# Mixture-of-experts stage: order of the gather products, layout of the down weights, one more place in the weight ring

## The chip, the core and the metric

The kernel runs on one core of a Trainium2 chip. Its metric is the device time of one execution in microseconds. The core has TensorE (matmul, in the profile PE, its weight loads PEld), VectorE (DVE), ScalarE (ACT), GpSimd (POOL) and SyncE (SP); SP issues nearly all transfers from HBM, in its program's order. "MB" here is 1024 KB.

## The reference, cut to what matters

Two blocks over 256 tokens of 1024 columns in float32. The first block ends in a mixture of 32 experts of which each token takes four:

```python
hf = h.reshape(T, D)                                    # 256 x 1024
logits = hf @ w_router + b_router
top_val, top_idx = lax.top_k(logits, 4)
gates = jax.nn.softmax(top_val, axis=-1)
...
gu = xb @ w_gu[e] + b_gu[e]                             # rows of expert e; w_gu[e] is 1024 x 2048
g = jnp.minimum(gu[:, :1024], 7.0)
u = jnp.clip(gu[:, 1024:], -7.0, 7.0)
act = (u + 1.0) * (g * jax.nn.sigmoid(1.702 * g))
return act @ w_dn[e] + b_dn[e]                          # w_dn[e] is 1024 x 1024
...
y = jax.ops.segment_sum(out * row_gate, row_tok)        # back to the tokens, weighted by the gates
```

Ahead of it stand attention, a state-space mixer and their projections; behind it two further layers.

## The kernel before, in words

Each expert has 64 slots for its tokens; a token's slot is its rank among the expert's tokens, and `S` (built on VectorE, L1205) is the 0/1 matrix from tokens to the slots of two neighbouring experts (a pair). All experts are run, so the stage reads all weights: 256 loads of 1 MB of `w_gu` and 128 MB of `w_dn`.

**An expert**, in TensorE's order, which is written out by hand in `moe` (L1296 to L1313, kept by `in_order`):

- `gate_up(j, ...)` for j = 1 to 7 (j = 0 was done during the expert before): one load of 128 rows of `w_gu` (128 partitions x 2048 columns, 8 KB a partition), four matmuls of 128x64 against 128x512 into the accumulators `pg` and `pu` (L1361; the profile counts two instructions for each float32 matmul). After j = 2 and 3 it scatters the expert before back to the tokens (L1427 to L1430, added to `x` on VectorE). After j = 5 the bias is added (L1364).
- `turn`: the transposed slot matrix and the gates by slot (L1373, L1376).
- `rows` gathers half of the columns (four blocks of 128) of the next pair: for each block two products of `xn` and `S` into a quarter of the accumulator `hg_p` (L1214), then a ScalarE copy with scale and bias into `hg` (L1215). An even expert gathers blocks 0 to 3 of the next pair, an odd one blocks 4 to 7.
- `act`: the activation on VectorE and ScalarE (`swiglu`, L1098 to L1102), four transposes of its column blocks `act[:, q*128:(q+1)*128]` (L1387) and a ScalarE copy `aT` (L1389). The 64 slots of both column halves lie on 128 partitions, so block q holds rows 128q to 128q+127 of the upper half of the inner columns in one half of the partitions, and those of the lower half in the other.
- `gate_up(0, ...)` of the next expert.
- `down`: four loads of two row blocks of `w_dn` (L1395; partition p gets row p of each block, 4 KB apiece; the last expert cuts the fourth in two), 16 matmuls into `pdn` (L1399), then `out` on VectorE and ScalarE (L1413 to L1415).

Before expert 6 stands the bias of the down products (`down_bias`, L1320), before expert 18 a branch (`overflow`, L1446) that all engines take past code for experts with more than 64 tokens.

**Transfers.** A load takes the next place of a ring of 1 MB places (`slot`, L285; `ring_use`, L172) and is issued by SP when TensorE has released that place. The mixer leaves seven places, the pool `wr` five, the mixer's own tiles three, and `moe` opens `RF` = 4 more: 19. The four are the last in the ring's order. Loads of the first expert start while the mixer's last projections run.

**On-chip memory.** `e32` (softmax of the router's values), `Gx` and `no` (overflow) and `ov_o` have tiles of their own.

Of the kernel before, what the change touches and what calls it, by code (L numbers as in the profile page):

```python
# [8 lines left out]
F32 = mybir.dt.float32  # L9
# [3 lines left out]
AF = mybir.ActivationFunctionType  # L13
OP = mybir.AluOpType
AX = mybir.AxisListType
# [4 lines left out]
T, D, NB = 256, 1024, 2  # L20
# [1042 lines left out]
BS = 1  # L1063
# [6 lines left out]
BR = 1  # L1070
BW = 1
WY = 0
RF = 4
SP = ()
W0 = 0
LT = 0
# [10 lines left out]
NE = 32  # L1087
# [94 lines left out]
def moe(k):  # L1182
    nc, tc, i = k.nc, k.tc, k.i
    ctx = ExitStack()
    ps, sm = k.ps, k.phase(ctx, "smE", 0)
    M = ctx.enter_context(tc.tile_pool(name="moe", bufs=1, reuse_waits="tile"))
    w_gu, b_gu, w_dn, b_dn = i["w_gu"][0], i["b_gu"][0], i["w_dn"][0], i["b_dn"][0]
    k.ring(RF)
    k.anchor = k.after
    k.ring_use(RU, [n for n in range(len(k.more)) if n not in RU])  # L1190

    rs, lg, G, sel, rk, v8 = k.rsx, k.lg, k.G, k.sel, k.rk, k.v8
# [16 lines left out]
    def rows(S, hg, half):  # L1209

        p = ps.tile([128, 4, 2 * SLOTS], F32, name="hg_p", tag="at", bufs=2)
        for j in range(4 * half, 4 * half + 4):
            for b in range(NB):
                nc.tensor.matmul(p[:, j % 4], xn[:, b, j * 128:(j + 1) * 128], S[:, b], start=b == 0, stop=b == 1)  # L1214
            k.lastg = nc.scalar.activation(hg[:, j], p[:, j % 4], AF.Identity, scale=k.Af[:, j:j + 1], bias=k.Bf[:, j:j + 1]).ins  # L1215

    def room_rows():
# [23 lines left out]
    hold.__enter__()  # L1241


    e32 = sm.tile([128, NB, NE], F32, name="rt_e", bufs=1)
    s1 = sm.tile([128, NB], F32, name="rt_s", bufs=1)
    nc.vector.tensor_tensor(e32, lg, v8[:, :, 0:1].to_broadcast([128, NB, NE]), op=OP.subtract)
    nc.scalar.activation(e32, e32, AF.Exp)
    nc.vector.tensor_tensor(e32, e32, sel, op=OP.mult)
    nc.vector.tensor_reduce(s1, e32, axis=AX.X, op=OP.add)
    nc.vector.reciprocal(s1, s1)  # L1250
    nc.vector.tensor_tensor(G, e32, s1[:, :, None].to_broadcast([128, NB, NE]), op=OP.mult)
    pn = ps.tile([128, 32], F32, name="pn", tag="at", bufs=2)
    for b in range(NB):
        nc.tensor.matmul(pn, k.ones, sel[:, b], start=b == 0, stop=b == 1)
# [13 lines left out]
    for m in range(2):  # L1268
# [4 lines left out]
        p = ps.tile([128, 512], F32, name="pb", tag="at", bufs=2)  # L1273
# [10 lines left out]
    for e in range(NE):  # L1284
        q, u = e // 2, e % 2
# [54 lines left out]
class Expert:  # L1340
# [41 lines left out]
    def act(self):  # L1382
        k, nc = self.k, self.k.nc
        act = swiglu(k, self.M, self.pg, self.pu, WE[0] if self.final else 0)
        pt = k.ps.tile([128, 4, 2, 64], F32, name="pat", tag="tr", bufs=2)
        for q in range(4):
            k.tr(pt[:, q].rearrange("p a s -> p (a s)"), act[:, q * 128:(q + 1) * 128])  # L1387
        self.aT = self.M.tile([128, 4, 2, 64], F32, name="aT", tag="su", bufs=BSU)
        nc.scalar.activation(self.aT, pt, AF.Copy, scale=0.5)  # L1389

    def down(self):
        k, nc, e = self.k, self.k.nc, self.e
        self.pd = pd = k.ps.tile([128, 512], F32, name="pdn", tag="at", bufs=2)
        for j0, jn in ((0, 2), (2, 2), (4, 2), (6, 1), (7, 1)) if self.final else ((0, 2), (2, 2), (4, 2), (6, 2)):
            w = k.load([(lambda t: t, self.w_dn[e, j0 * 128:(j0 + jn) * 128, :].rearrange("(k p) c -> p k c", p=128))],  # L1395
                       [128, jn, 1024])
            for j in range(j0, j0 + jn):
                for c in range(2):
                    nc.tensor.matmul(pd[c * 64:c * 64 + 64], self.aT[:, j % 4, j // 4], w[:, j - j0, c * 512:(c + 1) * 512],  # L1399
                                     start=j == 0, stop=j == 7)  # L1400
# [39 lines left out]
def overflow(k, M, xn, G, rk, cnt, cmi):  # L1440

    nc, tc, i = k.nc, k.tc, k.i
    ps, sm = k.ps, k.sm
    w_gu, b_gu, w_dn = i["w_gu"], i["b_gu"], i["w_dn"]
    go = nc.values_load(cmi[0:1, 0:1], min_val=0, max_val=T)
    with tc.If(go > SLOTS):  # L1446
        Gx = M.tile([128, NB, NE], F32, name="Gx")
        no = M.tile([128, 1], F32, name="no")
        nc.vector.tensor_scalar(Gx, rk, float(SLOTS), None, op0=OP.is_gt)
        nc.vector.tensor_tensor(Gx, Gx, G, op=OP.mult)  # L1450
        nc.vector.memset(no, 0.0)
        hF = k.slot([128, 8, 256], "ov_h")
        for j in range(8):
            p = ps.tile([128, 256], F32, name="ov_x", tag="at", bufs=2)
            for b in range(NB):
                k.tr(p[:, b * 128:(b + 1) * 128], xn[:, b, j * 128:(j + 1) * 128])
            nc.scalar.activation(hF[:, j], p, AF.Identity, scale=k.Af[:, j:j + 1], bias=k.Bf[:, j:j + 1])
        with tc.For_i(0, NE, 1) as e:
            nc.vector.tensor_scalar(no, no, 1.0, None, op0=OP.add)
            ce = nc.values_load(cnt[0:1, bass.ds(e, 1)], min_val=0, max_val=T)  # L1460
            with tc.If(ce > SLOTS):
                aT = k.slot([128, 8, 256], "ov_a")
                for f in range(2):
                    pp = [[ps.tile([128, 512], F32, name="ov_p", tag="mm", bufs=4) for b in range(NB)] for m in range(2)]
                    for m in range(2):
                        c0 = m * 1024 + f * 512
                        br = M.tile([1, 512], F32, name="ov_w", tag="st", bufs=BST)
                        nc.sync.dma_start(br, b_gu[0, bass.ds(e, 1), c0:c0 + 512])
                        for b in range(NB):
                            nc.tensor.matmul(pp[m][b], k.ones[0:1], br, start=True, stop=False)  # L1470
                        for j in range(8):
                            w = M.tile([128, 512], F32, name="ov_w", tag=("sg", "su", "st")[j % 3], bufs=(BSG, BSU, BST)[j % 3])
                            nc.sync.dma_start(w, w_gu[0, bass.ds(e, 1), j * 128:(j + 1) * 128, c0:c0 + 512]
                                              .rearrange("o p c -> p (o c)"))
                            for b in range(NB):
                                nc.tensor.matmul(pp[m][b], hF[:, j, b * 128:(b + 1) * 128], w, start=False, stop=j == 7)
                    for b in range(NB):
                        act = swiglu(k, M, pp[0][b], pp[1][b])
                        pt = ps.tile([128, 4, 128], F32, name="ov_t", tag="tr", bufs=2)
                        for q in range(4):  # L1480
                            k.tr(pt[:, q], act[:, q * 128:(q + 1) * 128])
                        nc.scalar.activation(aT[:, f * 4:f * 4 + 4, b * 128:(b + 1) * 128], pt, AF.Copy, scale=0.5)
                gc = sm.tile([128, NB], F32, name="ov_g", bufs=1)
                for b in range(NB):
                    oh = sm.tile([128, 32], F32, name="ov_o", bufs=2)
                    nc.vector.scalar_tensor_tensor(oh, k.c("iota")[:, 0:32], no, Gx[:, b], op0=OP.is_equal, op1=OP.mult,
                                                   accum_out=gc[:, b:b + 1])
                for c in range(2):
                    pd = [ps.tile([128, 512], F32, name="ov_d", tag="mm", bufs=4) for b in range(NB)]
                    for j in range(8):  # L1490
                        w = M.tile([128, 512], F32, name="ov_w", tag=("st", "su")[j % 2], bufs=(BST, BSU)[j % 2])
                        nc.sync.dma_start(w, w_dn[0, bass.ds(e, 1), j * 128:(j + 1) * 128, c * 512:(c + 1) * 512]
                                          .rearrange("o p c -> p (o c)"))
                        for b in range(NB):
                            nc.tensor.matmul(pd[b], aT[:, j, b * 128:(b + 1) * 128], w, start=j == 0, stop=j == 7)
                    gr = M.tile([128, 512], F32, name="ov_r", tag="sg", bufs=BSG)
                    nc.sync.dma_start(gr, bass.AP(tensor=k.gfd.tensor, offset=k.gfd.offset + c * 512, ap=[[0, 128], [1, 512]]))
                    for b in range(NB):
                        t = M.tile([128, 512], F32, name="ov_y", tag="su", bufs=BSU)
                        nc.vector.scalar_tensor_tensor(t, pd[b], gc[:, b:b + 1], gr, op0=OP.mult, op1=OP.mult)  # L1500
                        xx = k.x[:, b, c * 512:(c + 1) * 512]
                        nc.vector.tensor_tensor(xx, xx, t, op=OP.add)
# [559 lines left out]
```

## Time and profile before

| what | value |
|---|---|
| median of 3 runs | 2073.04 us (2069.82 to 2073.42) |
| the profiled execution | 2070.68 us |
| its span, first to last instruction | 2068.9 us |
| mean granted TensorE clock | 0.970 of full |
| busy: PE / PEld / DVE / ACT / POOL | 1913.7 / 1232.0 / 1058.5 / 759.4 / 214.0 us |
| moved from HBM | 583.21 MB (here 10^6 bytes) in 204331 packets, 171424 of them under 8 KB |

The busy time of an engine is an average over stages with different limits. A slice of the page's second part is 1/40 of the span, 51.7 us; the expert stage lies in slices 8 to 26. A line of a timeline gives start, duration, engine, source line, operation, and in brackets the idle time before it and what ended it. A float32 matmul counts as two instructions.

### The profile page before, as it was taken

How to read it: one execution, taken by the hardware profiler on the slowest of the kernel's cores; microseconds unless marked ns; L12 is line 12 of the kernel's file. 1: busy time of each engine (PE TensorE's matmuls, PEld its weight loads, DVE VectorE, ACT ScalarE, POOL GpSimd, SP SyncE). 2: the span in 40 equal slices, each digit the busy share in tenths (PEclk: the TensorE clock that was granted, in tenths of full speed). 3: DMA queues.
4: the chain of work that ended last, by engine and by line, in shares of the span. 5: the costliest groups of instructions: out<-in, count | busy, mean ns of one | idle time of the engine just before them, and what ended most of it. 6: DMA issues, size and time to landing. Idle time of an engine off the chain costs nothing.

```text
span 2068.9 us, 28319 instructions
## 1 busy us (share of the span) xinstructions
PE 1913.7 (92%) x11058; PEld 1232.0 (60%) x11059; DVE 1058.5 (51%) x1916; ACT 759.4 (37%) x1477; POOL 214.0 (10%) x379
## 2 busy tenths in 40 slices
PE   6898999999999999979999999899899999989998
PEld 4777888333333333323333333477699977769996
DVE  3788665222322222212222222387789757778984
ACT  3647444211101111101111111246567644556763
POOL 1324300000000000000000000111112101011210
PEclk9899999999999999989999999899999999999999
DMA  9766457999999999999999999453255546335552
GB/s 335 243 222 219 158 189 292 363 417 417 416 389 418 416 416 418 416 380 417 415 416 417 417 416 416 155 184 102 82 184 184 174 140 205 102 102 170 179 176 98
DMA packets 204331, 583.21 MB, mean 282 GB/s; under 512 B 15080, under 2 KB 92408, under 8 KB 171424
## 3 DMA queue, kind: packets, MB, share of 16 engines
q1 hardware_dynamic: 203200, 578.32, 73.7%
q0 software_dynamic: 704, 1.98, 0.3%
q8 instruction: 89, 1.46, 0.3%
q10 hardware_dynamic: 288, 1.05, 0.1%
q14 instruction: 50, 0.41, 0.1%
HBM read 580.23 MB, written 1.07 MB: 281 GB/s over the span
## 4 chain that ended last, share of the span: by engine, by line
PE 46%; DVE 5%; ACT 2%; issue 2%; DMA 1%; POOL 0%; DVEq 0%; POOLq 0%; ACTq 0%
PE mm L340 8%; PE mm L341 8%; PE mm L339 8%; PE pg L1361 5%; PE pu L1361 5%; PE pdn L1399 5%; PE hg_p L1214 2%; DVE wL L328 1%; ACT hg L1215 1%; PE pc L1427 1%; DVE ac L1870 1%; PE apv L1851 1%; ACT wH L327 0%; PE warm L403 0%; PE apl L1829 0%
## 5 line engine op out<-in xcount | busy, mean ns | idle before, releaser
L328 DVE TENSOR_TENSOR wL<-w,wH 128x1024 fp32r<-128x1024 f32 (+1 forms) x241 | 307.1, 1275 | 125.7 <-ACT wH L327 121.9
L327 ACT ACTIVATE wH<-w 128x1024 fp32r<-128x1024 f32 x259 | 272.0, 1052 | 181.9 <-PE mm L340 78.0
L1361 PE MATMUL pg<-w,hg 128*64 128x512 f32 x1024 | 280.2, 626 | 9.9 <-DMA w<-in_w_gu_dram 9.9
L1361 PE MATMUL pu<-w,hg 128*64 128x512 f32 x1024 | 267.1, 598 | 0.0
L341 PE MATMUL mm<-hnH,wL 128*128 128x256 f32 x800 | 229.1, 286 | 1.2 <-POOL xp L1865 0.8
L1399 PE MATMUL pdn<-w,aT 128*64 128x512 f32 x1024 | 225.2, 592 | 1.4 <-ACT aT L1389 1.4
L339 PE MATMUL mm<-hnH,wH 128*128 128x256 f32 x800 | 226.4, 283 | 0.0
L340 PE MATMUL mm<-hnL,wH 128*128 128x256 f32 x800 | 226.2, 283 | 0.0
L1413 DVE SCALAR_TENSOR_TENSOR oe<-pdn,gs,gf 128x512 f32<-128x512 f32 x32 | 24.0, 750 | 384.5 <-PE pdn L1399 384.5
L1099 ACT ACTIVATE sw_t<-sw_g 128x512 f32<-128x512 f32 x32 | 20.2, 630 | 424.7 <-DVE sw_g L1098 424.7
L1361 PEld LDWEIGHTS pu<-w,hg 128*64 128x64 f32 x1024 | 75.7, 141 | 154.0 <-issue 154.0
L1399 PEld LDWEIGHTS pdn<-w,aT 128*64 128x64 f32 x1024 | 72.9, 137 | 147.7 <-issue 144.5
L341 PEld LDWEIGHTS mm<-hnH,wL 128*128 128x128 f32 x800 | 153.2, 191 | 3.5 <-DVE wL L328 1.3
L339 PEld LDWEIGHTS mm<-hnH,wH 128*128 128x128 f32 x800 | 153.3, 192 | 0.5 <-issue 0.4
L340 PEld LDWEIGHTS mm<-hnL,wH 128*128 128x128 f32 x800 | 153.3, 192 | 0.0
L1214 PE MATMUL hg_p<-S,xn 128*128 128x128 f32 x512 | 94.2, 310 | 50.9 <-ACT hg L1215 49.3
L1361 PEld LDWEIGHTS pg<-w,hg 128*64 128x64 f32 x1024 | 63.6, 140 | 126.4 <-issue 121.8
L1430 DVE TENSOR_TENSOR x<-x,pc 128x512 f32<-128x512 f32 x128 | 82.5, 684 | 106.7 <-PE pc L1428 106.7
L1414 ACT ACTIVATE oeH<-oe 128x512 fp32r<-128x512 f32 x32 | 20.2, 630 | 293.7 <-DVE oe L1413 293.7
L1214 PEld LDWEIGHTS hg_p<-S,xn 128*128 128x128 f32 x512 | 69.3, 197 | 71.3 <-ACT hg L1215 66.9
L341 PE MATMUL mm<-hH,wL 128*128 128x256 f32 x320 | 96.3, 302 | 10.4 <-DVE wL L328 10.4
L328 POOL TENSOR_TENSOR wHL<-w,wHL 128x1024 fp32r<-128x1024 f32 x1 | 2.4, 2357 | 966.9 <-ACT wHL L327 966.9
(543 smaller groups left out, 3509.2 us busy)
## 6 DMA issues: line engine op xcount, KB each, us to landing
w<-in_w_gu_dram SPq DMA_DIRECT2D x256, 1024.0 KB, 13.8
w<-in_w_dn_dram SPq DMA_DIRECT2D x127, 1024.0 KB, 16.0
w<-in_w_in_dram SPq DMA_DIRECT2D x51, 1024.0 KB, 5.6
w<-in_w_up_dram SPq DMA_DIRECT2D x44, 1024.0 KB, 5.1
w<-in_w_down_dram SPq DMA_DIRECT2D x20, 1024.0 KB, 5.0
ad_l<-in_w_ada_dram SPq DMA_DIRECT2D x32, 512.0 KB, 4.3
w<-in_w_out_dram SPq DMA_DIRECT2D x12, 1024.0 KB, 5.1
w<-in_w_ada_dram SPq DMA_DIRECT2D x8, 1024.0 KB, 9.8
```

The source lines that it names most:

```text
L327: self.nc.scalar.activation(H, w, AF.Copy)
L328: (eng or self.nc.vector).tensor_tensor(L, w, H.bitcast(F32), op=OP.subtract)
L339: nc.tensor.matmul(out, sH, mH, start=start, stop=False, **kw)
L340: nc.tensor.matmul(out, sH, mL, start=False, stop=False, **kw)
L341: return nc.tensor.matmul(out, sL, mH, start=False, stop=stop, **kw)
L1214: nc.tensor.matmul(p[:, j % 4], xn[:, b, j * 128:(j + 1) * 128], S[:, b], start=b == 0, stop=b == 1)
L1215: k.lastg = nc.scalar.activation(hg[:, j], p[:, j % 4], AF.Identity, scale=k.Af[:, j:j + 1], bias=k.Bf[:, j:j + 1]).ins
L1361: nc.tensor.matmul(p[o:o + 64], hg, w[:, n * 512:(n + 1) * 512], start=j == 0, stop=j == 7 and e > 0)
L1399: nc.tensor.matmul(pd[c * 64:c * 64 + 64], self.aT[:, j % 4, j // 4], w[:, j - j0, c * 512:(c + 1) * 512], start=j == 0, stop=j == 7)
L1413: nc.vector.scalar_tensor_tensor(oe, self.pd, self.gs, k.gf, op0=OP.mult, op1=OP.mult)
L1427: nc.tensor.matmul(p, self.ST[o, b], self.oH[o], start=True, stop=False)
L1430: dx = nc.vector.tensor_tensor(xx, xx, p, op=OP.add)
```

## The change

- In `rows` the eight products of a half come first, then its four copies.
- `down` gives each partition two neighbouring rows of a 256-row block (8 KB in one piece in HBM) in place of one row from each of two 128-row blocks. So that products and weights meet, the transposes take every second column of a 256-column block: `act[:, c:c+255:2]`.
- `RF` goes from 4 to 5: 20 places.
- Memory for it: the softmax works in place in `G`; `Gx` and `no` take rooms of tiles that exist; `ov_o` has one buffer.

```diff
-RF = 4
+RF = 5
...
         for j in range(4 * half, 4 * half + 4):
             for b in range(NB):
                 nc.tensor.matmul(p[:, j % 4], xn[:, b, j * 128:(j + 1) * 128], S[:, b], start=b == 0, stop=b == 1)
+        for j in range(4 * half, 4 * half + 4):
             k.lastg = nc.scalar.activation(hg[:, j], p[:, j % 4], AF.Identity, scale=k.Af[:, j:j + 1], bias=k.Bf[:, j:j + 1]).ins
...
-    e32 = sm.tile([128, NB, NE], F32, name="rt_e", bufs=1)
...
-    nc.vector.tensor_tensor(e32, lg, v8[:, :, 0:1].to_broadcast([128, NB, NE]), op=OP.subtract)
-    nc.scalar.activation(e32, e32, AF.Exp)
+    nc.vector.tensor_tensor(G, lg, v8[:, :, 0:1].to_broadcast([128, NB, NE]), op=OP.subtract)
+    nc.scalar.activation(G, G, AF.Exp)
...
         for q in range(4):
-            k.tr(pt[:, q].rearrange("p a s -> p (a s)"), act[:, q * 128:(q + 1) * 128])
+
+            c = q // 2 * 256 + q % 2
+            k.tr(pt[:, q].rearrange("p a s -> p (a s)"), act[:, c:c + 255:2])
...
         for j0, jn in ((0, 2), (2, 2), (4, 2), (6, 1), (7, 1)) if self.final else ((0, 2), (2, 2), (4, 2), (6, 2)):
-            w = k.load([(lambda t: t, self.w_dn[e, j0 * 128:(j0 + jn) * 128, :].rearrange("(k p) c -> p k c", p=128))],
-                       [128, jn, 1024])
+            r = j0 // 2 * 256
+            src = self.w_dn[e, r:r + 256, :].rearrange("(p k) c -> p k c", k=2)
+            w = k.load([(lambda t: t, src[:, j0 % 2:j0 % 2 + jn])], [128, jn, 1024])
...
-        Gx = M.tile([128, NB, NE], F32, name="Gx")
-        no = M.tile([128, 1], F32, name="no")
+        Gx = M.tile([128, NB, NE], F32, name="Gx", tag="ST", bufs=BS)
+        no = M.tile([128, 1], F32, name="no", tag="gs", bufs=2)
...
-                    oh = sm.tile([128, 32], F32, name="ov_o", bufs=2)
+                    oh = sm.tile([128, 32], F32, name="ov_o", bufs=1)
```

## Rows read from the trace of the kernel before

**Rows 1.** Page, part 2: GB/s of the DMA engines in 40 slices.
```profile
GB/s 335 243 222 219 158 189 292 363 417 417 416 389 418 416 416 418 416 380 417 415 416 417 417 416 416 155 184 102 82 184 184 174 140 205 102 102 170 179 176 98
```

**Rows 2.** Waits of SP, whole span: us in total, times, longest.
```profile
SPq L301 <- PE pu L1361: 422.0, 177, 8.9
...
SPq L301 <- DMA w<-in_w_gu_dram: 82.0, 51, 2.4
```

**Rows 3.** TensorE timeline at expert 18: start, us, operation [idle before <-releaser].
```profile
912.28 1.12 PE L1361 MATMUL pg<-w,hg 128*64 128x512 f32 x2 [9.90 <-DMA w<-in_w_gu_dram]
```

**Rows 4.** ScalarE timeline, activation of experts 9, 10, 11 and 31.
```profile
649.38 0.63 ACT L1099 ACTIVATE sw_t<-sw_g 128x512 f32<-128x512 f32 x1 [12.86 <-DVE sw_g L1098]
...
678.06 0.63 ACT L1099 ACTIVATE sw_t<-sw_g 128x512 f32<-128x512 f32 x1 [12.86 <-DVE sw_g L1098]
...
708.36 0.63 ACT L1099 ACTIVATE sw_t<-sw_g 128x512 f32<-128x512 f32 x1 [12.86 <-DVE sw_g L1098]
...
1304.95 0.63 ACT L1099 ACTIVATE sw_t<-sw_g 128x512 f32<-128x512 f32 x1 [12.86 <-DVE sw_g L1098]
```

**Rows 5.** SP timeline, last expert load; landing of the issues from 1276 to 1284.
```profile
1281.45 2.09 SPq L301 DMA_DIRECT2D w<-in_w_dn_dram  x1
...
DMA to landing us min/median/max: 17.3/18.3/20.1
```

**Rows 6.** TensorE and VectorE timeline, end of expert 31.
```profile
1308.75 7.09 PE L1399 MATMUL pdn<-w,aT 128*64 128x512 f32 x32 [0.69 <-ACT aT L1389]
...
1315.89 0.75 DVE L1413 SCALAR_TENSOR_TENSOR oe<-pdn,gs,gf 128x512 f32<-128x512 f32 x1 [8.60 <-PE pdn L1399]
```

**Rows 7.** Timeline: a gather inside expert 0, then expert 1's, all engines.
```profile
359.53 1.16 PE L1214 MATMUL hg_p<-S,xn 128*128 128x128 f32 x8
360.62 1.08 PE L1361 MATMUL pg<-w,hg 128*64 128x512 f32 x4
...
409.22 0.46 ACT L1215 ACTIVATE hg<-hg_p,Bf,Af 128x128 f32<-128x128 f32 x1 [0.43 <-PE hg_p L1214]
...
409.73 0.71 PE L1214 MATMUL hg_p<-S,xn 128*128 128x128 f32 x4 [0.55 <-ACT hg L1215]
...
410.02 0.69 DVE L1102 SCALAR_TENSOR_TENSOR sw_t<-sw_t,sw_u 128x512 f32<-128x512 f32 x1
...
412.80 0.60 PE L407 MATMUL pat<-cst,sw_t 128*128 128x128 f32 x4
...
413.44 0.60 ACT L1389 ACTIVATE aT<-pat 128x512 f32<-128x512 f32 x1
...
415.10 7.04 PE L1399 MATMUL pdn<-w,aT 128*64 128x512 f32 x32
```

**Rows 8.** Waits of TensorE, whole span.
```profile
PE hg_p L1214 <- ACT hg L1215: 49.3, 90, 0.6
```

**Rows 9.** TensorE timeline behind the gather of expert 5.
```profile
530.18 1.12 PE L1361 MATMUL pg<-w,hg 128*64 128x512 f32 x2
```

**Rows 10.** SP timeline, four issues in a row late in the stage.
```profile
1235.92 0.33 SPq L301 DMA_DIRECT2D w<-in_w_gu_dram  x1
...
1238.48 0.33 SPq L301 DMA_DIRECT2D w<-in_w_gu_dram  x1
...
1241.01 0.33 SPq L301 DMA_DIRECT2D w<-in_w_gu_dram  x1
...
1243.50 0.38 SPq L301 DMA_DIRECT2D w<-in_w_dn_dram  x1
```

**Rows 11.** Stretches: us, busy us (instructions) of each engine, PEclk, DMA share, GB/s.
```profile
360.00:370.00 10.00, 10.00 (x57) 4.67 (x57) 1.66 (x8) 2.93 (x7) 0.00 (x0) 1.00 0.91 323
380.00:390.00 10.00, 8.35 (x46) 4.19 (x47) 1.39 (x4) 2.52 (x6) 0.00 (x0) 1.00 0.52 201
570.00:580.00 10.00, 10.00 (x48) 3.23 (x46) 1.44 (x2) 0.63 (x1) 0.00 (x0) 1.00 0.80 293
900.00:910.00 10.00, 1.84 (x5) 0.79 (x4) 2.48 (x4) 0.00 (x0) 0.00 (x0) 0.55 0.61 224
```

More of the change, by code (lines that the diff above doesn't have):

```diff
@@ L1241, in moe @@
     hold.__enter__()
-    e32 = sm.tile([128, NB, NE], F32, name="rt_e", bufs=1)
     s1 = sm.tile([128, NB], F32, name="rt_s", bufs=1)
-    nc.vector.tensor_tensor(e32, lg, v8[:, :, 0:1].to_broadcast([128, NB, NE]), op=OP.subtract)
-    nc.scalar.activation(e32, e32, AF.Exp)
-    nc.vector.tensor_tensor(e32, e32, sel, op=OP.mult)
-    nc.vector.tensor_reduce(s1, e32, axis=AX.X, op=OP.add)
+    nc.vector.tensor_tensor(G, lg, v8[:, :, 0:1].to_broadcast([128, NB, NE]), op=OP.subtract)
+    nc.scalar.activation(G, G, AF.Exp)
+    nc.vector.tensor_tensor(G, G, sel, op=OP.mult)
+    nc.vector.tensor_reduce(s1, G, axis=AX.X, op=OP.add)
     nc.vector.reciprocal(s1, s1)
-    nc.vector.tensor_tensor(G, e32, s1[:, :, None].to_broadcast([128, NB, NE]), op=OP.mult)
+    nc.vector.tensor_tensor(G, G, s1[:, :, None].to_broadcast([128, NB, NE]), op=OP.mult)
     pn = ps.tile([128, 32], F32, name="pn", tag="at", bufs=2)
```

## The prediction, made before the changed kernel ran

> **What bounds the kernel now.** I read the slices of the span first, then the expert stage alone: intervals between experts, waits of TensorE, waits of the DMA queue, spacing of its issues, stretches of 10 us. In the slices the expert stage is the plateau near 417 GB/s [rows 1]. The weights are 384 MB, the rate hardly leaves that plateau, and one would call the stage bound by transfers. It is not. SP waits for release of a place by TensorE (422.0 us in 177 waits) far more than for an earlier transfer (82.0 us) [rows 2]: the ring is full and TensorE empties it. TensorE waits for weights once in the stage, 9.90 us at the branch before expert 18 [rows 3], where all engines jump over the overflow code; I read that wait as the jump's and expect it to stay.
>
> TensorE's pace is in the start times of one ScalarE instruction that each expert issues once: 649.38 to 678.06 is 28.68 us, 678.06 to 708.36 is 30.30 us [rows 4]. Of the 31 intervals eight are of the long kind, 1.63 us longer. Twelve transfers of about 2.5 us are 30.1 us, so TensorE eats weights faster than they come. It never starved because its own stalls (the bias step after expert 5, the branch, the long intervals) let the ring fill again. At the end the last half megabyte is issued near 1281.5; the last four loads take 17.3 us and more to land [rows 5], so it is there at about 1299. TensorE is done with it at 1315.9 [rows 6]. Some 16 us of slack is therefore all that TensorE can gain before transfers take over, plus what transfers themselves can gain.
>
> **The change, part by part.**
>
> *Gather first, copies behind.* Now each of the four groups of products waits 0.55 us for the copy of the one before, and groups start 1.26 us apart; expert 0's first gather, where nothing waits, shows eight instructions in 1.09 us, 0.545 a group [rows 7]. Thirty gathers have 90 such waits, 49.3 us [rows 8]. Without them a gather is 4 x 0.545 = 2.2 us instead of 3 x 1.26 + 0.55 = 4.3, so 2.1 us shorter. What comes next may be late: the transposes need the activation, ready at 410.02 + 0.69 = 410.71, and products would end at 408.47 + 2.2 = 410.67 (the group before the row at 409.73 began 1.26 earlier): no loss. Then ScalarE has four copies of 0.46 us in a row, 1.84 us, and the copy of the transposed activation behind them: it would start near 412.7 and end near 413.3. The down products want to start 2.30 us behind the transposes (415.10 less 412.80), at 413.0 [rows 7]. So 0.3 to 0.6 us go back; where this copy has no cover now, TensorE waits 0.69 us for it [rows 6]. I take 1.7 us an expert; the ends are 0.5 (the copies also start late and cover nothing) and 2.1 (they start early).
>
> *The clock.* The long intervals have a stretch right behind the gather where two matmul instructions of 128x512 take 1.12 us [rows 9]; 32 of that shape take 7.09 us at the end of the stage [rows 6], 0.44 for two, so this is the lower level, 1.2 GHz. TensorE had just idled 0.55 of each 1.26 us. With the idle gone I take these eight as gone, 8 x 1.63 = 13 us; the other end is that all stay, 0.
>
> TensorE's own demand thus falls by 30 x 1.7 + 13 = 64 us, past the slack. From there transfers decide, so their sum is the forecast.
>
> *Two rows to a partition.* Late in the stage landings pace the issues: each issue waits for the landing of the one eight places back (up to 20.1 us in flight [rows 5], at 2.5 us each). The issues of the last gate-up loads thus show down-weight landings, 2.56 and 2.53 us apart, and the first down issue follows at 2.49, a gate-up landing [rows 10]. Gate-up rows are 8 KB in one piece, down rows 4 KB. The change makes down weights 8 KB a partition; I take 2.49 for them: 0.065 x 4 x 30 experts = 8 us less transfer time. Ends: 0 (the pieces stay 4 KB) and 9. The price is the transposes reading every second column. No row shows such a read of a stationary operand; the bounds are 0 and a doubling of the 0.60 us group [rows 7]; I take 0, and with 0.6 TensorE still has some 2 us an expert in hand against transfers.
>
> *The twentieth place.* It puts one more transfer, 2.5 us, in front while the ring is full. Against 417 GB/s the stretches 360 to 370, 380 to 390, 570 to 580 and 900 to 910 lose 2.3, 5.2, 3.0 and 4.6 us of transfer time [rows 11], because TensorE released nothing for a while. Of the first two the extra place regains 2.5 and the shorter gather 1.7. The other two vanish: by then TensorE is further ahead and some eight transfers are queued, and the same two stalls don't drain them. Sum 4.2 + 3.0 + 4.6 = 11.8 us; ends: 8 (only the later two) and 15 (all).
>
> *The rest.* In-place softmax issues the same instructions and ends long before its gate is read by the first expert. The overflow tiles lie in code that is jumped over. The extra place is the last in the ring's order, so a late release of its memory would delay only the load that now waits for expert 0 anyway. No load's queue or order changes otherwise.
>
> *Sum.* Last landing 1299 - 8 - 11.8 = 1279. The last gate-up load lands four transfers (10 us) earlier; behind it TensorE has one step of 1.7 us, 3.8 us to the down products (1304.95 [rows 4] to 1308.75), and 7.1 us of these [rows 6], which ends 2.6 us behind the last landing. I add 1.5 us because TensorE works off a few landed loads at that point. End 1283 instead of 1315.9: 33 us. The layers behind it start 33 us earlier with unchanged work; their first load is next in the same queue. The profiled execution took 2070.68 us, span 2068.9: 2070.7 - 33 = 2038. The median shown is 2.4 us above that execution, so I state 2038 with the spread of such runs inside the range.
>
> **The rivals.**
>
> *Down pieces stay as they are* (their two rows not joined into one piece): 8 us fewer, 2046. For it: nothing in the trace shows joined rows. Against: each partition's two rows are adjacent on both sides.
>
> *The wait only moves and TensorE stays the bound*: saving 0.5 us an expert and the clock still falling, 30 x 0.5 = 15 us, 2056. For it: ScalarE's four copies now stand ahead of the one that the down products need. Against: these have 2.3 us of cover.
>
> *Nothing*: the tool that orders the instructions keeps the copies interleaved or the strided transposes eat the gain; 2070.
>
> *Slower: the clock.* Once TensorE is ahead it waits for weights in each expert, about 29.8 - 27.0 = 2.8 us. If that drops the clock twice in each expert at 1.63 us, TensorE takes 30 x (3.3 - 1.7) = 47 us more, less the 13 us of drops that it has now: 34 us slower, 2105. It decides from 1.3 drops an expert (2.1 us saved, the present drops among it, over 1.63). For it: after the 9.9 us idle at the branch the granted clock of that stretch was 0.55 [rows 11], and gathers with 44% idle drop it in eight cases. Against: those gathers did not in 23 others, and a slowed TensorE stops waiting, so the cause removes itself. The Trainium skill (TensorE: Matmul & The Clock Gate, "HAM oscillation") says that a loop which computes for less time than it waits for its next weights is throttled again in every tile; by that rule the risk is real only where waits are longer than the work, which no row before shows: here the wait would be 2.8 of 29.8 us. I leave it 9 in 100.
>
> **How the numbers follow.** Transfers become the bound: 0.66, 2031 to 2044, likeliest 2038. Pieces stay: 0.10. Wait moves: 0.10. Nothing: 0.05. Clock: 0.09. The range 2030 to 2058 holds the first three and leaves out the last two; its low end is the sum of the better ends (15 + 9 regained, nothing to work off: 2032) less 2 us for the spread of runs. Changes of under 0.2% (4 us) are what this measurement can't tell from none: faster 0.86, same 0.05, slower 0.09.
>
> **What would show it.** The waits of the gather products for ScalarE are gone and groups are 0.55 us apart; intervals start near 27 us and settle near 29.8 once waits for gate-up weights of 2 to 3 us appear in each expert. SP waits for landings rather than releases in the second half; issues are 2.49 apart throughout; packets under 8 KB become fewer. The last load lands near 1279, the last down products end near 1283. I am wrong if intervals stay at 28 us or more from the start (moved wait, clock), if TensorE never waits for weights, or if the half-speed stretches multiply.

## The result, and the profile after

The changed kernel takes 2042.49 us (median of 4 runs, 2040.89 to 2043.66) against 2071.43 us of the kernel before (4 runs, 2066.49 to 2073.42) beside it on the same chip: a ratio of 0.986 [0.985, 0.988], 29 us less. The forecast was 2038 and 33 us; the result lies in the range, and in the direction and the case (transfers become the bound) that were called likeliest. The profiled execution took 2042.99 us with a span of 2041.3.

First the page, the GB/s of the 40 slices and the packets:

```profile
GB/s 339 238 228 211 167 179 288 390 420 421 420 420 420 420 420 420 421 375 420 420 420 420 420 420 420 241 145 93 82 213 177 176 153 191 104 83 176 187 175 93
...
DMA packets 188075, 583.21 MB, mean 286 GB/s; under 512 B 15080, under 2 KB 92408, under 8 KB 138912
```

Against [rows 1] the expert stage has one dip left (375, the branch); the dip of 389 is gone, and the plateau stands at 420 instead of 417. The packets fit the two rows to a partition: under 8 KB there are 138912, and 171424 where the down weights have the old layout (the page of the kernel with the order alone, below).

Next the waits, of SP (three rows) and of TensorE: us in total, times, longest.

```profile
SPq L301 <- DMA w<-in_w_gu_dram: 449.6, 215, 3.2
...
SPq L301 <- DMA w<-in_w_dn_dram: 224.8, 105, 6.0
...
SPq L301 <- PE pu L1361: 67.6, 41, 8.7
...
PE pg L1361 <- DMA w<-in_w_gu_dram: 20.7, 40, 0.7
```

SP's waits have changed sides [rows 2]: 422.0 us for TensorE's release became 67.6, and 82.0 us for an earlier gate-up transfer became 449.6, with 224.8 for down transfers. TensorE waits for gate-up weights 40 times, half a microsecond on average and never over 0.7 us. Its 90 waits for a copy inside a gather [rows 8], three in each of 30 gathers, are gone.

The timeline of the stage, in order of time: start, us, engine and operation [idle before it, and what ended it].

```profile
354.59 5.44 PE L1214 MATMUL hg_p<-S,xn 128*128 128x128 f32 x32 [1.40 <-DVE S L1205]
...
571.89 2.05 PE L1214 MATMUL hg_p<-S,xn 128*128 128x128 f32 x16
...
573.98 1.51 ACT L1216 ACTIVATE hg<-hg_p,Bf,Af 128x128 f32<-128x128 f32 x4 [1.77 <-PE hg_p L1214]
...
574.27 0.72 PE L407 MATMUL pat<-cst,sw_t 128*128 128x128 f32 x4 [0.33 <-DVE sw_t L1102]
...
575.36 0.61 ACT L1391 ACTIVATE aT<-pat 128x512 f32<-128x512 f32 x1
...
576.68 1.89 PE L1402 MATMUL pdn<-w,aT 128*64 128x512 f32 x8
...
624.43 0.63 ACT L1099 ACTIVATE sw_t<-sw_g 128x512 f32<-128x512 f32 x1 [12.86 <-DVE sw_g L1098]
...
651.28 0.63 ACT L1099 ACTIVATE sw_t<-sw_g 128x512 f32<-128x512 f32 x1 [12.86 <-DVE sw_g L1098]
...
677.60 0.63 ACT L1099 ACTIVATE sw_t<-sw_g 128x512 f32<-128x512 f32 x1 [12.85 <-DVE sw_g L1098]
...
862.33 0.33 SPq L301 DMA_DIRECT2D w<-in_w_gu_dram  x1
...
864.83 0.33 SPq L301 DMA_DIRECT2D w<-in_w_dn_dram  x1
...
867.34 0.33 SPq L301 DMA_DIRECT2D w<-in_w_dn_dram  x1
...
1216.36 0.63 ACT L1099 ACTIVATE sw_t<-sw_g 128x512 f32<-128x512 f32 x1 [15.82 <-DVE sw_g L1098]
...
1246.47 0.63 ACT L1099 ACTIVATE sw_t<-sw_g 128x512 f32<-128x512 f32 x1 [16.05 <-DVE sw_g L1098]
...
1276.36 0.63 ACT L1099 ACTIVATE sw_t<-sw_g 128x512 f32<-128x512 f32 x1 [14.82 <-DVE sw_g L1098]
...
1280.25 7.09 PE L1402 MATMUL pdn<-w,aT 128*64 128x512 f32 x32 [0.69 <-ACT aT L1391]
...
1287.39 0.75 DVE L1416 SCALAR_TENSOR_TENSOR oe<-pdn,gs,gf 128x512 f32<-128x512 f32 x1 [8.68 <-PE pdn L1402]
```

What to see in it: the gather inside expert 7 (571.89) is one group of 2.05 us where [rows 7] had groups 1.26 us apart. The four copies take 1.51 us together, and the copy of the transposed activation ends at 575.97, ahead of the down products at 576.68, so these do not wait for ScalarE. The transposes wait 0.33 us for the activation here. Four transposes with the stride take 0.72 us, where [rows 7] had 0.60. The intervals between the activations are 26.85 and 26.32 us around 650 us, where [rows 4] had 28.68 and 30.30, and 30.11 and 29.89 at the end, where transfers pace. SP's issues around a down piece are 2.50 and 2.51 us apart; [rows 10] had 2.56 and 2.53. The last down products begin at 1280.25 instead of 1308.75 [rows 6], 28.5 us earlier, and that is the gain: from there to the end both profiles take about as long (760.2 and 761.1 us of their spans).

Now the stretches that [rows 11] showed, with 370 to 380 beside them and the 100 us around the branch; the last two columns are the DMA share and GB/s, the one before them the granted clock:

```profile
360.00:370.00 10.00, 10.00 (x45) 3.51 (x46) 2.30 (x11) 2.82 (x8) 0.00 (x0) 1.00 1.01 389
...
370.00:380.00 10.00, 10.00 (x61) 4.66 (x58) 2.33 (x6) 1.50 (x3) 0.00 (x0) 1.00 0.96 375
...
380.00:390.00 10.00, 9.95 (x51) 3.92 (x51) 0.51 (x1) 1.99 (x5) 0.00 (x0) 1.00 0.97 351
...
570.00:580.00 10.00, 9.67 (x68) 5.21 (x66) 3.39 (x9) 2.95 (x7) 0.00 (x0) 1.00 1.01 418
...
900.00:910.00 10.00, 1.47 (x6) 1.02 (x8) 2.74 (x5) 2.63 (x7) 0.00 (x0) 0.50 0.56 206
...
860.00:960.00 100.00, 77.90 (x368) 29.79 (x366) 19.02 (x35) 7.74 (x17) 0.00 (x0) 0.85 0.96 398
```

Between 360 and 390 us the transfers now lose 3.4 us against 420 GB/s; before, they lost 2.3 and 5.2 in the two stretches of [rows 11] against 417, and 0.5 in the one between them (396 GB/s). The dip at 570 to 580 is gone. The one at 900 to 910 is still there: 206 GB/s, and 398 instead of 420 over 100 us, so 5.2 us lost. This is the branch before expert 18, seen by its own line (first and last start of each kind, then who waited for it):

```profile
L1449 SPq EVENT_SEMAPHORE  x9: 17/17/17, 890.6 to 905.3; - x9
...
L1449 PEldq COMPARE_BRANCH  x1: 5989/5989/5989, 868.3 to 868.3; - x1
...
L1449 SPq COMPARE_BRANCH  x1: 50/50/50, 885.5 to 885.5; - x1
...
  DVE sw_g L1098: 16.5, 1
```

SP reaches its branch at 885.5, has a last event there at 905.3, and issues nothing in those 20 us. That is how long one piece takes to land with eight on the way: its last issue ahead of the branch was near 885, and 19.9 us is the median landing time of a gate-up piece on the page. The events are those of the join, the point behind the skipped code where SP goes on. Of SP's waits from 880 to 912 us the join takes 19.4 us, and a release by TensorE 0.3 us:

```profile
SPq L1449 <- SPq L1449: 19.4, 3, 11.8
```

The drain costs the transfers less than its 20 us, because the eight pieces on the way still land. The rate is full until about 899 us, falls while the queues run empty, and is full again at 908:

```profile
904.00:905.00 1.00, 0.00 (x0) 0.00 (x0) 0.00 (x0) 0.00 (x0) 0.00 (x0) 0.50 0.02 8
...
908.00:909.00 1.00, 0.47 (x3) 0.50 (x3) 0.39 (x1) 0.61 (x2) 0.00 (x0) 0.50 1.03 434
```

DVE's first step of expert 18 waits 16.5 us, until SP's join is over, TensorE's transposes wait for DVE (13.6 us), and the interval of this expert is 54.6 us.

### The profile page after: what moved, and what is told of

Read it like the earlier page. It is cut to its first block, busy times and chain, and to the rows that moved or that the text cites. A ratio compares the mean times of both kernels' runs of the same rounds, so it can differ in the third digit from the quotient of the medians.

```text
span 2041.3 us, 28318 instructions
## 1 busy us (share of the span) xinstructions
PE 1899.5 (93%) x11058; PEld 1223.8 (60%) x11059; DVE 1057.7 (52%) x1916; ACT 746.4 (37%) x1477; POOL 215.3 (11%) x379
## 2 busy tenths in 40 slices
DMA packets 188075, 583.21 MB, mean 286 GB/s; under 512 B 15080, under 2 KB 92408, under 8 KB 138912
## 4 chain that ended last, share of the span: by engine, by line
PE 34%; DMA 13%; DVE 5%; issue 2%; ACT 1%; POOL 0%; DVEq 0%; POOLq 0%; ACTq 0%; SPq 0%
DMA w<-in_w_gu_dram 9%; PE mm L340 8%; PE mm L341 8%; PE mm L339 8%; DMA w<-in_w_dn_dram 4%; PE pdn L1402 2%; PE pg L1361 2%; PE pu L1361 1%; DVE wL L328 1%; DVE ac L1873 1%; PE apv L1854 1%; PE apl L1832 1%; PE warm L403 0%; ACT wH L327 0%; PE po L1915 0%
## 5 line engine op out<-in xcount | busy, mean ns | idle before, releaser
L1361 PE MATMUL pu<-w,hg 128*64 128x512 f32 x1024 | 271.3, 599 | 0.0
L340 PE MATMUL mm<-hL,wH 128*128 128x256 f32 x320 | 95.2, 299 | 4.2 <-DVE hL L591 4.2
L339 PE MATMUL mm<-hH,wH 128*128 128x256 f32 x320 | 96.6, 303 | 1.6 <-ACT hH L589 1.2
## 6 DMA issues: line engine op xcount, KB each, us to landing
w<-in_w_gu_dram SPq DMA_DIRECT2D x256, 1024.0 KB, 19.9
w<-in_w_dn_dram SPq DMA_DIRECT2D x127, 1024.0 KB, 19.9
```

The source lines that it names most:

```text
L339: nc.tensor.matmul(out, sH, mH, start=start, stop=False, **kw)
L340: nc.tensor.matmul(out, sH, mL, start=False, stop=False, **kw)
L1361: nc.tensor.matmul(p[o:o + 64], hg, w[:, n * 512:(n + 1) * 512], start=j == 0, stop=j == 7 and e > 0)
```

## The experiments

What is compared is the time with its ratio to the kernel before, and, from each profile, the **length of the stage**: from the first product of the first gather to the start of the last down products, both in the timeline of TensorE. The length leaves out the layers in front, where one execution differs from the next: the first gather starts anywhere from 348.20 to 354.98 us. It has a weakness: where transfers decide, an execution that comes early to its gather has to wait the longer for the weights, so I take a length as good to some 3 us. It also comes from one profiled execution of each kernel, while the times are medians of four or five runs (twelve of the copies back). The kernel before ran again beside each group of experiments, with medians from 2068.97 to 2072.14 us, so rows of different groups are compared by their ratios: 0.001 is 2 us.

| kernel | us | ratio to before | gather | down | stage |
|---|---|---|---|---|---|
| before | 2071.43 | 1 | 354.29 | 1308.75 | 954.46 |
| changed | 2042.49 | 0.9863 [0.985, 0.988] | 354.59 | 1280.25 | 925.66 |
| copies back between products | 2070.71 | 0.9997 [0.999, 1.001] | 354.19 | 1310.59 | 956.40 |
| order alone | 2048.42 | 0.9885 [0.987, 0.990] | 354.17 | 1288.31 | 934.14 |
| changed, old down layout | 2047.67 | 0.9891 [0.988, 0.991] | 350.38 | 1284.10 | 933.72 |
| changed, 19 places | 2041.95 | 0.9855 [0.984, 0.987] | 354.98 | 1282.34 | 927.36 |
| changed, no branch | 2034.49 | 0.9834 [0.982, 0.985] | 348.20 | 1271.10 | 922.90 |
| changed, branch before 31 | 2049.55 | 0.9903 [0.989, 0.992] | 353.54 | 1286.97 | 933.43 |
| before, no branch | 2057.61 | 0.9939 [0.993, 0.995] | 353.58 | 1292.48 | 938.90 |
| changed, products twice | 2047.26 | 0.9894 [0.988, 0.991] | 352.42 | 1282.80 | 930.38 |
| changed, branch before 1 | 2050.82 | 0.9897 [0.988, 0.992] | 351.00 | 1284.00 | 933.00 |
| changed, branch before 8 | 2042.32 | 0.9861 [0.984, 0.988] | 351.98 | 1277.88 | 925.90 |

The theory: TensorE's demand set the pace before, the new order alone takes it below the transfers, and layout and place are worth something only then. The rival: layout and place carry the gain, since SP's ring covered the gather's waits. A second question is where the 4.5 us between forecast and result went.

**Copies back between the products** (layout and place stay).

```diff
@@ rows(), the changed kernel
-        for j in range(4 * half, 4 * half + 4):
             k.lastg = nc.scalar.activation(hg[:, j], p[:, j % 4], AF.Identity, ...
```

> The changed kernel with its eight copies between the products again; the down weights two rows to a partition and the twentieth place stay. If the order of the gather is what moved TensorE below the transfers: TensorE needs 28.7 us an expert again, 12 transfers of 2.49 us need 29.9 only in the odd stretch, hg_p waits on ACT hg return at about 49 us in 90 waits, and the time is 2064 to 2074 us. If the layout and the place carry the gain: 2045 to 2055 us.

Measured: 2070.71 us. The waits of TensorE and SP:

```profile
PE hg_p L1214 <- ACT hg L1215: 49.4, 90, 0.6
...
SPq L301 <- PE pu L1360: 562.0, 237, 9.0
```

The 90 waits are back with 49.4 us, SP waits for release again, and so are the long intervals: ten of 30.3 us among those of 28.7. Nothing is left of the gain, although pieces of 8 KB and the twentieth place are there. The rival falls: without the order the two other parts bring nothing.

**The order alone**, in the kernel before.

```diff
@@ rows(), the kernel before
+        for j in range(4 * half, 4 * half + 4):
             k.lastg = nc.scalar.activation(hg[:, j], p[:, j % 4], AF.Identity, ...
```

> The kernel before with nothing changed but the order of products and copies (19 places, down weights in the old layout). By the theory of the order most of the 29 us comes with this alone; missing are 0.06 us on each of 128 down pieces (8 us) and one place (2.5 us): 2050 to 2056 us, with down pieces spaced 2.55 us in stretches where transfers bound. If layout or place carry the gain: 2064 to 2072 us.

Measured: 2048.42 us. Two lines of the page:

```profile
GB/s 332 247 224 218 167 177 292 373 418 417 416 417 417 416 417 417 416 378 416 416 417 417 416 416 417 260 157 85 84 209 182 175 149 200 103 83 175 186 174 94
...
DMA packets 204331, 583.21 MB, mean 285 GB/s; under 512 B 15080, under 2 KB 92408, under 8 KB 171424
```

One line moved gives 20.3 of the 28.8 us in the stage. The plateau is there without its dip of 389, but at 416 to 417 instead of 420. The time is 1.6 us below the expected range; the stage is 8.5 us longer than the changed kernel's.

**The changed kernel with the old down layout** and plain transposes.

```diff
@@ Expert.act() and Expert.down(), the changed kernel
-            c = q // 2 * 256 + q % 2
-            k.tr(pt[:, q].rearrange("p a s -> p (a s)"), act[:, c:c + 255:2])
+            k.tr(pt[:, q].rearrange("p a s -> p (a s)"), act[:, q * 128:(q + 1) * 128])
...
-            r = j0 // 2 * 256
-            src = self.w_dn[e, r:r + 256, :].rearrange("(p k) c -> p k c", k=2)
-            w = k.load([(lambda t: t, src[:, j0 % 2:j0 % 2 + jn])], [128, jn, 1024])
+            w = k.load([(lambda t: t, self.w_dn[e, j0 * 128:(j0 + jn) * 128, :].rearrange("(k p) c -> p k c", p=128))],
+                       [128, jn, 1024])
```

> The changed kernel with the down weights of 4 KB runs and the plain transposes again; gather order and twentieth place stay. If transfers bound the weight stage and a down piece costs 0.06 us more in 4 KB runs: 128 x 0.06 = 8 us, of which what falls into stretches where TensorE bounds (about a third of the experts) is lost to neither: 2046 to 2051 us. Rival, that the pieces' length does not matter since TensorE still sets the pace, and that the transposes, which take 0.1 us more with the stride, come back: 2039 to 2043 us.

Measured: 2047.67 us. The two ends of the stage in the timeline:

```profile
350.38 5.44 PE L1214 MATMUL hg_p<-S,xn 128*128 128x128 f32 x32 [1.39 <-DVE S L1205]
...
1284.10 7.09 PE L1400 MATMUL pdn<-w,aT 128*64 128x512 f32 x32 [0.69 <-ACT aT L1390]
```

The stage is 933.72 against 925.66 us, 8.1 us longer, which over 128 MB of down weights is 0.063 us for each, near the term of the prediction (8 us from 0.065). The rates agree: 384 pieces of 1024 KB at 417 GB/s take 6.9 us longer than at 420. The ratios differ by 0.0028, 5.8 us, with an interval of some 3 us either way. A second pair, both with 19 places, is the order alone against the changed kernel with 19 places below: 6.5 us in the times and 6.8 in the stage. So the layout is worth 6 to 8 us, 0.045 to 0.063 us a piece. The Trainium skill (DMA: Bandwidth & Descriptors, "Why small descriptors are slow") gives each packet a fixed price of some 3 cycles on top of one cycle for 32 bytes. An estimate from that is 262 against 259 cycles for 8 KB, 1.2%; the runs show 0.045 to 0.063 in 2.49 us, 1.8 to 2.5%. The direction agrees, the size is larger, and the measurement decides.

**The changed kernel with 19 places.**

```diff
-RF = 5
+RF = 4
```

> The changed kernel with 19 places. Where transfers bound the place is worth one transfer of 2.5 us at the stretch before it, where the ring last stood full: 2044 to 2047 us. Rival, that the ring never runs full once transfers bound: 2042 us, no change. Second rival, that each of the ring's full stretches (360 to 390 us, and the branch) pays it again: 2048 us and more.

Measured: 2041.95 us, no different from the changed kernel's; the stage is 1.7 us longer, in an execution of 2047.12 us, the slowest of its four. The place does what it was read for where the ring is full: in the 10 us from the first gather the changed kernel (first line) moves 385 GB/s, the one with 19 places 279, a difference of 2.5 us at 420:

```profile
354.59:364.59 10.00, 10.00 (x52) 6.78 (x52) 1.77 (x8) 3.67 (x10) 0.00 (x0) 0.83 1.01 385
...
354.98:364.98 10.00, 10.00 (x52) 6.78 (x52) 1.77 (x8) 3.67 (x10) 0.00 (x0) 0.83 0.79 279
```

That gain lies inside the spread of the times. At the branch the kernel with 19 places shows a long wait:

```profile
903.05 1.97 PE L1361 MATMUL pg<-w,hg 128*64 128x512 f32 x4 [31.85 <-DMA w<-in_w_gu_dram]
```

With 19 places TensorE waits 31.85 us for weights at the branch, which it never does with 20, and still the stage ends only 1.7 us later. The order of SP's instructions around the branch explains the wait. This is the order in the built program, not a view of the profile, with 19 places (in the kernel before too):

```
317 L301 DMA w_6781<-in_w_gu_dram 128x2048
318 L301 DMA w_6787<-in_w_gu_dram 128x2048
319 L301 DMA w_6801<-in_w_gu_dram 128x2048
320 L1449 COMPARE_AND_BRANCH
...
440 L1449 UNCONDITIONAL_BRANCH [waits SP_sequencer_49,DMAHW0_49,DMAHW1_49,DMAHW2_49,DMAHW3_49,DMAHW4_49,DMAHW5_49,DMAHW6_49,DMAHW7_49]
441 L301 DMA w_6647<-in_w_gu_dram 128x2048 [waits DMAHW6_49]
442 L301 DMA w_6653<-in_w_gu_dram 128x2048 [waits DMAHW7_49]
```

The tiles are numbered in the order of the program. Two gate-up pieces of expert 18 (6647 and 6653) stand behind the branch, after pieces of expert 19: the overflow code takes two places of the ring, and here they are the two that these pieces get. With 20 places all twelve of expert 18 and six of expert 19 stand ahead. And line 440 waits for eight DMA semaphores of SP ahead of the join: SP goes on only when everything that it has issued is there. So much is in the code; the runs that follow price it.

**The changed kernel without the branch.** It leaves out the code for experts with more than 64 tokens, which these inputs do not enter.

```diff
         if e == OVER:
-            overflow(k, M, xn, G, rk, cnt, cmi)
             chain = {}
```

> The changed kernel without the code for experts with over 64 tokens and without its branch before expert 18; these inputs do not enter that code, and expert 17's scatter stays where it was. If the join at the branch makes SP wait until its own eight queues are empty, and transfers lose about 5 us by it (206 GB/s in the window 900 to 910), nothing is lost there without it: SP's L1449 waits are gone, spacing of the pieces stays at 2.49 us across expert 18, 2035 to 2039 us. Rival, that the ring's places ran out there since TensorE stood in the branch, or that the stall gave back stock that is needed later: 2041 to 2044 us.

Measured: 2034.49 us. Two stretches of 100 us, and TensorE's wait for weights:

```profile
860.00:960.00 100.00, 92.28 (x473) 33.86 (x473) 24.57 (x45) 10.73 (x24) 0.00 (x0) 1.00 1.01 420
...
1160.00:1260.00 100.00, 88.83 (x448) 31.00 (x444) 24.65 (x41) 9.55 (x21) 0.00 (x0) 1.00 1.01 420
```

```profile
PE pg L1360 <- DMA w<-in_w_gu_dram: 39.5, 72, 2.0
```

Where the changed kernel moved 398 GB/s around the branch, 420 are moved: the 5.2 us are back. The ratios differ by 0.0029, 6.0 us, with the interval of each some 3 us wide either way; the stage is only 2.8 us shorter, in an execution whose gather came 6.4 us early. So the place and the kind of the loss are shown, its size to a few us. This edit takes away the pauses of TensorE and DVE at the branch together with SP's drain; that it was SP which held the transfers up rests on SP's waits in the changed kernel, 19.4 us at the join against 0.3 for TensorE. The stretches show one thing more. TensorE waits for gate-up weights 72 times, 0.55 us on average and once 2.0 us, and the granted clock stays at 1.00.

**The branch before expert 31**, where all pieces are ahead of it.

```diff
-OVER = 18
+OVER = 31
```

> The changed kernel with its branch moved from before expert 18 to before expert 31, where all 385 pieces stand ahead of it in SP's order. If SP's drain at the join is the price, the transfers run on to the end without a gap and the last lands about 5 us earlier; TensorE pays its own 6 us in the branch so close to the end that it can win back only part of it: 2036 to 2043 us, likeliest 2039. Rival, that the branch costs the same wherever it stands: 2041 to 2044 us. Rival on the other side, that DVE's wait for the join (16.5 us before expert 18) now stands in front of the last expert and nothing hides it: 2046 to 2055 us.

Measured: 2049.55 us; the timeline:

```profile
1265.04 1.97 PE L1361 MATMUL pg<-w,hg 128*64 128x512 f32 x4 [6.48 <-PEq L1449]
...
1280.02 1.03 PE L1361 MATMUL pg<-w,hg 128*64 128x512 f32 x4
...
1286.97 7.09 PE L1402 MATMUL pdn<-w,aT 128*64 128x512 f32 x32 [0.69 <-ACT aT L1391]
```

The expectation of 2036 to 2043 us missed. The drain now falls where no expert's piece is left to issue, and the transfers run without a gap before it (the stretch 860 to 960 moves 421 GB/s). But TensorE comes out of its branch at 1265.04, after 6.48 us in it, works at the lower clock for a while (1.97 us for four products, 1.03 elsewhere) and gets to the last down products 7.8 us later in the stage than the changed kernel does. The rival of the other side had the sign and the size; its reason holds for a small part alone. DVE waits 23.3 us there, most of it for TensorE: the products that its step reads (`pg`) end at 1281.05, and the step starts at 1282.62, 0.3 us behind SP's last event at the join (1282.3). So the drain added at most some 1.5 us; the rest is TensorE's late start.

**The kernel before without the branch**, the same edit there.

> The kernel before without the overflow code and its branch. If TensorE set the pace there, what goes is TensorE's own loss at the branch, the interval of expert 18 falling from about 44 us to about 33 us: 10 to 12 us less, 2058 to 2064 us. If the transfers set it, only their 4.6 us go: 2065 to 2069 us.

Measured: 2057.61 us, 11.4 less than the 2068.97 of the kernel before in that batch; the interval of expert 18 falls from 46.2 to 30.0 us, and the stage is 15.6 us shorter. Where TensorE sets the pace the branch costs TensorE's stall; where transfers do, it costs what the drain takes from them.

**All products of a gather twice**, so that an expert takes longer on TensorE without any wait. The second set writes the same sums over the first.

```diff
@@ rows(), the changed kernel
-        for j in range(4 * half, 4 * half + 4):
+        for j in (*range(4 * half, 4 * half + 4), *range(4 * half, 4 * half + 4)):
             for b in range(NB):
```

> The changed kernel with all products of a gather issued twice, the second time over the first: 16 more records, 2.05 us more TensorE work an expert and no new wait, so that an expert needs about 28.6 us as in the kernel before, and no half clock. If TensorE's demand below the transfers' 29.9 us costs only where the ring stands full and the pause between two experts' products holds SP, a part of the 29 us comes back: 2050 to 2060 us. If work under 29.9 us is free, as the bound by transfers taken alone says: 2042 to 2045 us. If TensorE still set the pace everywhere: 2066 us and more.

Measured: 2047.26 us, between two of the expected bands; the timeline:

```profile
584.79 3.84 PE L1214 MATMUL hg_p<-S,xn 128*128 128x128 f32 x32
...
612.22 0.63 ACT L1099 ACTIVATE sw_t<-sw_g 128x512 f32<-128x512 f32 x1 [12.85 <-DVE sw_g L1098]
...
640.27 0.63 ACT L1099 ACTIVATE sw_t<-sw_g 128x512 f32<-128x512 f32 x1 [12.86 <-DVE sw_g L1098]
```

A gather takes 3.84 us instead of 2.05, and the interval is 28.05 us from 400 to 1220, but for the bias step and the branch, against a mean of 26.6; so 1.5 us an expert were added, not the 2.05 that I expected. Some 45 us more of TensorE work cost 4.7 us in the stage. Below about 28 us an expert TensorE's work is nearly free: that is where transfers take over. No interval is a long one, although TensorE does more: the lower clock comes with the waits inside a gather, not with the amount of work.

**The branch before expert 1 and before expert 8** (`OVER = 1`, `OVER = 8`).

> The changed kernel with its branch before expert 1, with 30 of the 385 pieces ahead of it. If the drain costs the transfers about 5 to 7 us wherever they run without a gap, it costs that here too, beside the ring's own full places between 360 and 390 us (389, 375 and 351 GB/s), which it may cover in part: 2038 to 2044 us. Rival, that a full ring around 380 us hides the drain altogether: 2034 to 2037 us. Rival on the other side, that TensorE, held for 16 us with the ring full, stops the transfers as well: 2048 us and more.

> The changed kernel with its branch before expert 8, with 114 pieces ahead of it, in the stretch where TensorE (26.6 us an expert) is faster than the transfers and lives on the stock. If the drain is the price, the same 5 to 7 us are lost here and no stock is wanted later that the stall could have given: 2039 to 2045 us, the same as before expert 18. Rival, that TensorE's stall is the price and early there is stock to spend: 2034 to 2038 us.

Measured: 2050.82 us before expert 1, 2042.32 before expert 8. Two stretches with the branch before expert 1:

```profile
380.00:390.00 10.00, 7.74 (x35) 2.59 (x32) 2.50 (x4) 0.63 (x1) 0.00 (x0) 0.94 0.91 328
...
390.00:400.00 10.00, 4.66 (x12) 1.79 (x13) 1.51 (x3) 0.00 (x0) 0.00 (x0) 0.50 0.59 231
```

There the ring is full when TensorE stops, so the two stretches move only 328 and 231 GB/s, and the stage is 7.3 us longer: the rival on the other side. Before expert 8 the stage is 925.90 us, the changed kernel's to 0.3 us: at the two places in the middle of the stage that were run, before 8 and before 18, the branch costs the same. No version with the overflow code in it beat the changed kernel beyond the noise. A branch ahead of the first expert, or fewer transfers on the way when SP reaches it, was not tried.

## Why the prediction was nearly right, and the step that failed

*The bound before* was read rightly: TensorE set the pace and some 16 us of slack hid the transfers. With the copies back between the products the full time returns.

*Gather first*: taken as 1.7 us an expert with ends 0.5 and 2.1; the intervals show 28.68 - 26.58 = 2.1, the upper end, with the price of the stride in it. The prediction speaks of a wait in each of four groups; its sum rightly has three, and so has the count of 90. The 0.3 to 0.6 us that the late copies were to give back are not seen in the gather shown: the four copies take 1.51 instead of 1.84 us, and the copy behind them ends before the down products want it.

*The clock*: all eight long intervals are gone, as taken (13 us); the kernel with the copies back has ten, those with the new order none of this kind. With 30 gathers, 22 others and not 23 kept the full clock before.

*Transfers decide from there*: right, and TensorE's waits came, but not as 2 to 3 us at once: they are pieces of about 0.5 us, some three in each expert that the transfers pace. TensorE's demand fell by about 30 x 2.1 + 13 = 76 us, 29 of which show. The run with doubled products measures the surplus from the other side.

*Two rows to a partition*: 8 us predicted, 6 to 8 found. The stride's price was taken as 0 and is 0.12 us for four transposes, which lies in TensorE's surplus.

*The twentieth place and what the ring loses*, 11.8 us, is where it failed. The parts at 360 to 390 (4.2 predicted; a loss of 8.0 us became one of 3.4) and at 570 to 580 (3.0, all regained) hold. The place itself, read as 2.5 us, is 2.5 behind the first gather, 1.7 in the stage and nothing that the times can show. The third, 4.6 us at 900 to 910, does not: "by then TensorE is further ahead and some eight transfers are queued, and the same two stalls don't drain them". It is not TensorE that stops the transfers at the branch but SP itself, whose join waits until its queues are empty. The trace of the kernel before has the join too, in the same stretch:

```profile
L1446 SPq EVENT_SEMAPHORE  x9: 17/17/17, 900.8 to 906.6; - x9
```

The prediction put this loss to TensorE, whose own pause ends there at the same time (906.7), so that trace alone could not tell the two apart. The loss of 4.6 us is now one of 5.2, and without the branch it is gone. The end shows the same shift: the last half piece is issued at 1267.05 and takes 17.4 us, so it lands near 1284.5 where 1279 was forecast, and the last down products end at 1287.3 instead of 1283. The sum with this term at nothing is 2042.6; measured 2042.5. That this fits to 0.1 us is luck: the runs spread over 2.8 us, and the other terms are known to a few us only.

A reading that failed without harm: the 9.90 us wait at the branch [rows 3] was put down to the jump and expected to stay. It came from two pieces of expert 18 that SP had behind its branch, and with 20 places they stand ahead. Nothing was won by it, since DVE's wait for the join took its place.

*The rivals*: pieces that stay, a wait that only moves, and no change are all excluded by the rows above. The clock rival (9 in 100) did not come true, but its condition was hardly met either: it wanted 2.8 us of idle time at once in each expert, and the run without the branch has 72 waits of 0.55 us on average, with a granted clock of 1.00 in the stretches shown. What one long wait in each expert would do, no run shows. In the changed kernel the clock does fall while TensorE waits, to 0.95 and 0.88 in the two stretches of 10 us from 1240 to 1260, but not in each expert, and the transfers set the end all the same. The Trainium skill (TensorE: Matmul & The Clock Gate, "HAM oscillation") speaks of loops that wait for longer than they work; here the work is far longer than the waits, so no run here tests its rule.

## What to carry to other kernels

A stage at its transfer rate on the page can still be paced by an engine: ask what SP waits for, releases or landings, before believing the GB/s. Group the products that feed one buffer and put the copies behind them; look for this first where two engines alternate on one accumulator, and expect the gain to stop where the next bound lies. A branch whose join drains a queue costs the time in which the queue runs empty and fills again, 5 us here in the middle of the stream, and more where an engine has no stock or no time left behind it: near either end of the stage it was 7 to 8 us dearer than in the middle.

## What the hardware did that was not expected

TensorE's row has 5.99 us for its compare-and-branch at L1449 (6.15 us before expert 31), SP 0.05 us for the same instruction. The Trainium skill (Runtime: NRT & Kernel Launch, "Instruction fetch mechanics") says that a taken branch beyond the instructions already fetched waits for a fetch. A row that long fits it, but no run here separates the fetch from other causes.

With three waits of 0.55 us in a gather, 1.26 us apart, the clock fell in eight to ten gathers of 30 and not in the others; which ones was not settled. Waits for weights of about 0.55 us, three or four spread over the 30 us of an expert, hardly ever went with a fall.

The profiled executions differ by up to 6.8 us in when the first gather starts. What a difference of 2 us between two kernels is worth, as that of the twentieth place, neither the time nor the length of the stage can settle.
